# The entry of a hybrid encoder step: four chunks instead of three for the first three weight tiles, and the norm written out part by part

## The chip, the cores and the metric

The kernel runs on one NeuronCore of one Trainium2 chip, in a single launch. The metric is device time in microseconds (us): 1714.21 us, median of three runs (1712.94 to 1715.49). TensorE does matrix products, VectorE (DVE) and ScalarE (ACT) elementwise work, GpSimd (POOL) slower elementwise work, and SyncE (SP) issues most DMAs. Tiles with 128 partitions hold the data; TensorE writes to PSUM banks of 128x512 fp32.

## The reference, cut to what matters

One layer of a hybrid trunk on 1024 prompt tokens and 32 sample tokens, width 1024:

```python
h = rmsnorm(x, ln_mix_g)                 # per token: x * rsqrt(mean(x*x) + 1e-6) * g
z = h @ w_in + b_in                      # 1024 -> 2952 columns, split among head groups
x += w_out @ concat[mLSTM(z), stick_breaking_attention(z), S5(z) + GLU]
x += cross_attention(rmsnorm(x), memory K/V)
x += conv_ffn(rmsnorm(x))
y = rmsnorm(x, ln_f_g)
```

Everything is fp32. The kernel gets fp32 accuracy from the faster fp32r matmul by splitting each operand into a high part (rounded to fp32r) and a low part (the rest): a product is hi·hi + hi·lo + lo·hi, three matmuls.

## The kernel before, in words

The change lies in the entry, the first 64 us, in which the norm of x and the first three weight tiles of `w_in` are worked through.

**Token tiles.** x comes in nine token tiles (eight of 128 tokens, one of 32), `xts[0]` to `xts[8]`, loaded by `x_load` (L584) on SP's queue. `norm_T` (L555) takes one tile through: ACT squares it and sums over the row (L563); DVE computes mean + eps (L565); POOL raises that to the power -1/2 (L566); DVE multiplies x by this factor and by the weight row `gmix` in one instruction over 1024 columns (L568); TensorE turns the tile in two halves of four 128x128 transposes (L574); ACT copies each half from PSUM to `h_hi` as fp32r (L575), and DVE subtracts that from the PSUM half to give `h_lo` (L576). `gmix` is the weight row `ln_mix_g` repeated on all 128 partitions, loaded by one DMA of 512 KB (L593).

**Weight tiles.** `WStream` (L384) loads tiles of 1024 rows x 128 columns (512 KB, `w_raw`, two buffers). `split` (L406) makes `w_hi` on ACT (L417) and `w_lo` by a subtraction, on POOL for the first three tiles and on DVE afterwards (L418). The third tile holds the eight gate columns, and its two parts lie side by side in one operand, so that it takes two matmuls per row block instead of three.

**The product.** `dense_cmajor` (L464) runs the first three weight tiles (`u` 0, `u` 1, gate) chunk by chunk: the tokens are cut at `IN_AT` = 0, 384, 768, 1056 (L41), and each chunk needs its token tiles (`need_h`, L1684). `group` (L439) does one weight tile on one chunk: eight row blocks, 24 matmuls (16 for the gate). `ev_in` (L713) takes the result from PSUM to SBUF and DRAM. All other 21 weight tiles of `w_in` follow tile by tile (`dense`, L455).

**What sets the order.** The functions are generators. A planner written in the kernel keeps a modelled time for each engine (`place`, L72; `Timed`, L132): main work is written out in order, and after every second row block `advance` (L234) lets each side job (`Side`, `Window`, L189 to L227) write its next step if the modelled TensorE time has come to the step's due time. `x_tile` for the nine tiles runs in such a window of four at a time (L1680); the weight vectors that are needed later (`vec_late`, L638), the S5 part, stick-breaking attention, mLSTM and the memory norm are added as side jobs after eight steps of the main loop (L1710). The framework's scheduler (switched on in L2517) then sets the final order on each engine, so an instruction that is written later can be issued earlier if it is ready in the scheduler's model: three S5 loads on ACT's queue are issued at 0.73 to 1.66 us though S5 is written much later.

**Queues.** SP issues, in the order written (L592 to L618): x tile 0, `gmix`, x tiles 1 and 2, weight tile 0, x tile 3, weight tile 1, two bias rows, the gate bias, the gate weights, x tiles 4 to 8.

Of the kernel before, what the change touches and what calls it, by code (L numbers as in the profile page):

```python
# [39 lines left out]
IN_ORDER = "b0 b1 a0 a1 b2 a2".split()  # L40
IN_AT = [0, 3 * P, 6 * P, TA]  # L41


# [10 lines left out]
def tile_fn(tc, *args):  # L54
# [77 lines left out]
    class Timed:  # L132
# [23 lines left out]
        def __getattr__(self, name):  # L156
            f = getattr(self.eng, name)

            def timed(*args, **kw):
# [13 lines left out]
                return f(*args, **kw)  # L173
            return timed

    v = Timed(nc.vector, "dve")
# [5 lines left out]
    def asf(ap):  # L182
        return ap.bitcast(F32)
# [77 lines left out]
    with ExitStack() as top:  # L261
# [104 lines left out]
        def const(shape, dt=F32, name="c"):  # L366
            return cpool.tile(shape, dt, name=name)
# [16 lines left out]
        class WStream:  # L384
# [51 lines left out]

        W = WStream()

        def group(w, mov, c, n, kt):  # L439
# [147 lines left out]

        def x_tile(i):
            yield from norm_T(None, P if i < 8 else TS, gmix, h_hi, h_lo, i * P, xts[i])
            xn[0] = i + 1  # L590

        x_load(0, sy)  # L592
        sy.dma_start(gmix, a["ln_mix_g"][0].partition_broadcast(P))  # L593
        x_load(1, sy)
        x_load(2, sy)
        W.load()
        x_load(3, sy)
        W.load()


# [6 lines left out]
        def rows(tl, at, ap):  # L607
            n = ap.shape[0] // P
            sy.dma_start(tl[at:at + n, :], ap.rearrange("(r c) -> r c", c=P))
            return at + n  # L610

        rows(ra, rows(ra, 0, a["b_in"][0, 0:1536]), a["b_in"][0, 1544:2952])
        bgate = const([36, 1], name="bgate")
        sy.dma_start(bgate[0:4, :], a["b_in"][0, 1536:1540].unsqueeze(1))
# [23 lines left out]
        def vec_late():  # L638
# [74 lines left out]
        def ev_in(jj, c, ps):  # L713
            key, j = order[jj]
            sl = slice(IN_AT[c], IN_AT[c + 1])
            w = IN_AT[c + 1] - IN_AT[c]
            rs_ = slice(j * P, (j + 1) * P)
            pv = ps[:, :w]
            if key == "u":
                if c == 0:  # L720
                    full[jj] = xb.tile([P, 8, NB], "ur")
                n0, nn = IN_AT[c] // 8, w // 8
                s.activation(full[jj][:, :, n0:n0 + nn], pv.rearrange("p (n t) -> p t n", t=8), AF.Identity,
                             bias=vecA[:, bias_at[key, j]:bias_at[key, j] + 1])
                if c == NCH - 1:
                    sy.dma_start(d_u[rs_], full[jj])
                    avail.add((key, j))
                return
            clear(1)
            st = sp.tile([P, IN_W], "stg")[:, :w]  # L730
            if key == "gate":
# [7 lines left out]
                sy.dma_start(d_g[4:8, sl], st[32:36, :])  # L739
                if c == NCH - 1:  # L740
                    avail.add(key)
# [13 lines left out]
            if key in ("qa", "ka"):  # L755
                sy.dma_start((d_qa if key == "qa" else d_ka)[rs_, sl], st)
                if c == NCH - 1:
                    ready_a.append((key, j))
            if key in ("kb", "vb", "va", "oa"):
# [3 lines left out]
                def later():  # L763
                    ps2 = tp()
                    b0, nb = IN_AT[c] // P, w // P
                    for i in range((w + P - 1) // P):
# [3 lines left out]
                    v.tensor_copy(nat[:, b0:b0 + nb, :], ps2[:, 0:nb, :])  # L770
                    if c == NCH - 1:
                        v.tensor_copy(nat[:TS, 8, :], ps2[:TS, nb, :])
# [902 lines left out]

        hm = lambda k, c: (h_hi[:, k, IN_AT[c]:IN_AT[c + 1]], h_lo[:, k, IN_AT[c]:IN_AT[c + 1]])
        in_n = [IN_AT[c + 1] - IN_AT[c] for c in range(NCH)]
        chunks = list(range(NCH))
        h_free = []
        xw_ = add(Window((x_tile(i) for i in range(9)), 4))  # L1680
        until(lambda: xn[0] >= 1)
        W.prime(1)

        def need_h(c):  # L1684
            until(lambda: xn[0] * P >= min(IN_AT[c + 1], T) and (c < 2 or xn[0] == 9))

# [25 lines left out]
        drive(dense(len(order) - 3, hm, chunks, in_n, lambda j, c, ps: ev_in(j + 3, c, ps)))  # L1712
        clear(0)
# [807 lines left out]
```

## Time and profile before

| what | value |
|---|---|
| median of three runs | 1714.21 us |
| profiled execution, its own time | 1716.38 us |
| its span | 1714.6 us |
| granted TensorE clock, mean | 0.987 |
| PE busy | 1642.7 us, 96% of the span |
| DVE busy | 1137.3 us, 66% |
| ACT busy | 753.6 us, 44% |
| POOL busy | 463.2 us, 27% |

The profile is of one execution. Busy times of PE overlap from one matmul to the next, so the spacing of two starts tells a matmul's cost, not its duration. A row of the timeline gives the start and the length in us, the engine, the output and the inputs, the shape, how many instructions were merged, and in brackets how long the engine had been idle and what ended that. Tiles appear under the names of the memory zones in which they lie: `zb` holds `h_hi`, `za` holds `h_lo`, `zf` x tiles 0 to 3, `zy` x tiles 4 to 8, `zr` the gate weights' two parts.

### The profile page before, as it was taken

To read this page: it belongs to the slowest core of one execution; us is meant where nothing else is said; L and a number is where in the kernel's file an instruction comes from. 1 tells how busy PE (TensorE), PEld (TensorE's weight loads), DVE (VectorE), ACT (ScalarE), POOL (GpSimd) and SP (SyncE) were. 2 spreads that over 40 slices of the span, in tenths; PEclk is the share of its full clock that TensorE was granted. 3 is DMA by queue.
4 is the path that set the end of the run, shared out by engine and by line. 5 is a ranking of instruction groups with operands and counts; after the bars stand their busy time and mean duration, and the time that the engine had idled before them with its cause. 6 is when DMAs were issued, how large, how long until landed. Compare 5 with 4: busy or idle time off the path is not lost.

```text
span 1714.6 us, 30434 instructions
## 1 busy us (share of the span) xinstructions
PE 1642.7 (96%) x11616; PEld 1598.1 (93%) x11616; DVE 1137.3 (66%) x2209; ACT 753.6 (44%) x1480; POOL 463.2 (27%) x624
## 2 busy tenths in 40 slices
PE   5999999999999799999999989999999999999997
PEld 5989989999888799999999889999999999999997
DVE  6778878845796667766656698777777777333232
ACT  5434434534664555544444454444444445111143
POOL 4234335011214233200102546533333330000022
PEclk9999999999899999999999999999999999999999
DMA  7564544254479965455554555222222217332121
GB/s 216 146 161 115 138 109 105 78 158 133 124 232 257 253 200 162 125 170 178 171 167 124 159 158 169 94 76 89 86 75 75 76 63 240 127 100 75 43 69 65
DMA packets 328392, 229.91 MB, mean 134 GB/s; under 512 B 43564, under 2 KB 309707, under 8 KB 327991
## 3 DMA queue, kind: packets, MB, share of 16 engines
q1 hardware_dynamic: 309991, 214.57, 42.5%
q10 hardware_dynamic: 18256, 13.40, 2.6%
q8 instruction: 92, 1.51, 0.4%
q14 instruction: 53, 0.43, 0.1%
HBM read 170.95 MB, written 56.38 MB: 133 GB/s over the span
## 4 chain that ended last, share of the span: by engine, by line
PE 76%; DMA 9%; DVE 8%; issue 2%; ACT 2%; POOL 1%; SPq 1%; ACTq 0%; DVEq 0%; POOLq 0%
PE mm L173 47%; PE gp L173 19%; PE tp L173 10%; DVE zy L173 3%; DVE zf L173 2%; DVE zr L173 1%; DVE zx L173 1%; DMA d_mv<-zr 1%; DMA zf<-d_act 1%; SPq L173 1%; DVE w_lo L173 1%; DMA w_raw<-in_w_in_dram 1%; ACT zy L173 1%; DMA zy<-d_uu 1%; ACT zf L173 0%
## 5 line engine op out<-in xcount | busy, mean ns | idle before, releaser
L173 PE MATMUL mm<-zb,w_hi 128*128 128x352 f32 (+4 forms) x1234 | 366.5, 330 | 2.5 <-DVE zb L173 1.3
L173 PE MATMUL mm<-zr,w_hi 128*128 128x352 f32 (+2 forms) x1358 | 289.2, 312 | 8.4 <-ACT zf L173 4.1
L173 ACT ACTIVATE w_hi<-w_raw 128x1024 fp32r<-128x1024 f32 (+1 forms) x150 | 149.6, 997 | 284.5 <-PE mm L173 207.2
L173 PE MATMUL mm<-zb,w_lo 128*128 128x384 f32 (+2 forms) x826 | 273.6, 331 | 0.0
L173 POOL TENSOR_TENSOR zf<-zf 128x352 f32<-128x352 f32 (+5 forms) x98 | 118.5, 1210 | 566.5 <-ACT zf L173 484.8
L173 PE MATMUL mm<-zr,w_lo 128*128 128x264 f32 (+2 forms) x1058 | 235.9, 304 | 0.7 <-ACT zf L173 0.7
L173 PEld LDWEIGHTS mm<-zb,w_hi 128*128 128x128 f32 x1234 | 227.6, 190 | 4.3 <-DVE zb L173 1.6
L173 PEld LDWEIGHTS mm<-zr,w_hi 128*128 128x128 f32 x1358 | 216.2, 191 | 10.8 <-ACT zf L173 4.8
L173 DVE TENSOR_TENSOR w_lo<-w_raw,w_hi 128x1024 fp32r<-128x1024 f32 (+1 forms) x127 | 159.8, 1258 | 55.8 <-ACT w_hi L173 55.1
L173 PE MATMUL mm<-za,w_hi 128*128 128x384 f32 (+1 forms) x552 | 184.5, 334 | 0.0
L173 DVE TENSOR_TENSOR zx<-mm,zx 128x352 f32<-128x352 f32 (+3 forms) x120 | 62.7, 523 | 177.7 <-PE mm L173 177.3
L173 PEld LDWEIGHTS mm<-zr,w_lo 128*128 128x128 f32 x1058 | 164.6, 189 | 0.9 <-ACT zf L173 0.9
L173 PEld LDWEIGHTS mm<-zb,w_lo 128*128 128x128 f32 x826 | 157.8, 191 | 0.7
L173 PE MATMUL tp<-ident,zf 128*128 128x128 f32 (+3 forms) x530 | 89.1, 285 | 31.1 <-DVE zf L173 22.2
L173 PE MATMUL mm<-zy,w_hi 128*128 128x352 f32 x456 | 114.1, 326 | 1.6 <-DVE zx L173 1.6
L173 PE MATMUL gp<-zy 128*128 128x132 f32 (+13 forms) x722 | 109.7, 290 | 2.2 <-DVE zg L173 0.9
L173 DVE TENSOR_TENSOR zy<-zy 128x16 f32<-128x16 f32 (+9 forms) x371 | 97.5, 304 | 15.3 <-POOL zy L173 6.7
L173 ACT ACTIVATE zf<-gp 128x512 f32<-128x512 f32 (+6 forms) x180 | 75.6, 476 | 72.2 <-PE gp L173 59.6
L173 PEld LDWEIGHTS mm<-za,w_hi 128*128 128x128 f32 x552 | 106.4, 193 | 0.5
L173 PEld LDWEIGHTS tp<-ident,zf 128*128 128x128 f32 (+3 forms) x530 | 64.3, 146 | 41.7 <-DVE zf L173 20.8
L173 PEld LDWEIGHTS gp<-zy 128*128 128x128 f32 (+6 forms) x722 | 97.1, 186 | 4.9 <-DVE zg L173 1.3
L173 POOL TENSOR_TENSOR zy<-zy 128x16 f32<-128x16 f32 (+8 forms) x123 | 82.3, 680 | 67.7 <-DVE zy L173 56.9
(232 smaller groups left out, 3364.2 us busy)
## 6 DMA issues: line engine op xcount, KB each, us to landing
w_raw<-in_w_ffn_a_dram SPq DMA_DIRECT2D x27, 512.0 KB
w_raw<-in_w_out_dram SPq DMA_DIRECT2D x24, 512.0 KB
w_raw<-in_w_xq_dram SPq DMA_DIRECT2D x24, 512.0 KB
w_raw<-in_w_xo_dram SPq DMA_DIRECT2D x24, 512.0 KB
w_raw<-in_w_in_dram SPq DMA_DIRECT2D x23, 512.0 KB
d_act<-zx SPq DMA_DIRECT2D x22, 528.0 KB
zf<-d_act SPq DMA_DIRECT2D x22, 528.0 KB
w_raw<-in_w_ffn_down_dram SPq DMA_DIRECT2D x16, 512.0 KB
```

The source lines that it names most:

```text
L173: return f(*args, **kw)
```

## The change

- `IN_FIRST` = 0, 256, 512, 768, 1056: the first three weight tiles run over four chunks of two token tiles each (the last also has the 32 sample tokens). The other weight tiles keep `IN_AT`.
- The 512 KB load of `gmix` is gone. One row of 4 KB is loaded into a corner of `xts[7]`, TensorE multiplies a column of ones by it into two PSUM banks (`gps`), tiles 0 and 1 are scaled from PSUM, and ACT copies `gps` to `gmix` for the other tiles.
- SP's order is x 0, the weight row, x 1, the bias rows, weight tiles 0 and 1, x 2, x 3, then the rest as before.
- The norm is written out as parts (`squares`, `factor`, `scaled`, `turned`, `low`), for tiles 0 and 1 in a fixed interleaving, for the others in a generator that works on three tiles at a time. `keep` ties each of these instructions on ACT and DVE behind the one kept before on the same engine.
- `w_lo` of weight tile 0 is made on POOL in four quarters, of weight tile 1 on DVE in the kept order, of the gate tile on DVE.
- `vec_late` waits until 12 us of modelled TensorE time have gone by before it writes its two transposes, and these keep their place in the written order.

```diff
+IN_FIRST = [0, 2 * P, 4 * P, 6 * P, TA]
+    kept = {}
+    def keep(eng, name, *args, **kw):
+        if eng.key in kept:
+            with tc.issue_after(kept[eng.key]):
+                r = getattr(eng, name)(*args, **kw)
+        else:
+            r = getattr(eng, name)(*args, **kw)
+        kept[eng.key] = r.ins
...
-                s.activation(hi[:, :kt, :cols], raw[:, :kt, :cols], AF.Copy)
-                (v if self.at + len(self.ready) > 2 else g).tensor_tensor(
-                    out=lo[:, :kt, :cols], in0=raw[:, :kt, :cols], in1=asf(hi[:, :kt, :cols]), op=ALU.subtract)
+                if self.at + len(self.ready) < 2:
+                    keep(s, "activation", hi[:, :kt, :cols], raw[:, :kt, :cols], AF.Copy)
+                    if self.at + len(self.ready) == 0:
+                        for k in range(0, kt, 2):
+                            g.tensor_tensor(out=lo[:, k:k + 2], in0=raw[:, k:k + 2], in1=asf(hi[:, k:k + 2]),
+                                            op=ALU.subtract)
+                    else:
+                        keep(v, "tensor_tensor", out=lo[:, :kt, :cols], in0=raw[:, :kt, :cols],
+                             in1=asf(hi[:, :kt, :cols]), op=ALU.subtract)
+                else:
+                    s.activation(hi[:, :kt, :cols], raw[:, :kt, :cols], AF.Copy)
+                    v.tensor_tensor(out=lo[:, :kt, :cols], in0=raw[:, :kt, :cols], in1=asf(hi[:, :kt, :cols]),
+                                    op=ALU.subtract)
...
         x_load(0, sy)
-        sy.dma_start(gmix, a["ln_mix_g"][0].partition_broadcast(P))
+        grow = xts[7][0:1, :]
+        sy.dma_start(grow, a["ln_mix_g"][0].unsqueeze(0))
         x_load(1, sy)
-        x_load(2, sy)
-        W.load()
-        x_load(3, sy)
-        W.load()
         rows(ra, rows(ra, 0, a["b_in"][0, 0:1536]), a["b_in"][0, 1544:2952])
+        W.load()
+        W.load()
+        x_load(2, sy)
+        x_load(3, sy)
+        gps = [gp() for _ in range(2)]
+        for q in range(2):
+            pe.matmul(gps[q], ones4[0:1, :], grow[:, 512 * q:512 * q + 512], start=True, stop=True)
...
-            yield
+            t = clk["pe"]
+            while clk["pe"] < t + 12:
+                yield
             pa, pb = gp(), gp()
-            pe.transpose(pa[:, :34], ra[:34], ident[:34, :34])
-            pe.transpose(pb[:, :88], rb, ident[:88, :88])
+            tc.keep_in_program_order(pe.transpose(pa[:, :34], ra[:34], ident[:34, :34]))
+            tc.keep_in_program_order(pe.transpose(pb[:, :88], rb, ident[:88, :88]))
...
+        squares(0)
+        squares(1)
+        factor(0)
+        scaled(0, 0)
+        factor(1)
+        scaled(0, 1)
+        p00, p01 = turned(0, 0), turned(0, 1)
+        scaled(1, 0)
+        low(0, 0, p00)
         W.prime(1)
+        scaled(1, 1)
+        low(0, 1, p01)
+        p10, p11 = turned(1, 0), turned(1, 1)
+        low(1, 0, p10)
+        low(1, 1, p11)
+        xn[0] = 2
+        for q in range(2):
+            keep(s, "activation", gmix[:, HALF[q]], gps[q], AF.Copy)
+
+        def others():
+            for i in range(2, 11):
+                if i < 9:
+                    squares(i)
+                if 2 <= i - 1 < 9:
+                    scaled(i - 1)
+                if i < 9:
+                    factor(i)
+                yield
+                for q in range(2) if 2 <= i - 2 < 9 else ():
+                    low(i - 2, q, turned(i - 2, q))
+                    if q:
+                        xn[0] = i - 1
+                    yield
...
-        main = dense_cmajor(3, hm, chunks, in_n, ev_in, need_h)
+        main = dense_cmajor(3, hm(IN_FIRST), range(4), in_n(IN_FIRST), ev_in, need_h)
```

`squares`, `factor`, `scaled`, `turned` and `low` are L563, L565 with L566, L568, L574 with L575, and L576 of `norm_T`, with ACT's and DVE's instructions under `keep`; `scaled` of tiles 0 and 1 works on halves of 512 columns and reads `gps`, of the others on 1024 columns and reads `gmix`. `ev_in` takes its cuts from `IN_FIRST` for the first three weight tiles and asks for the last chunk by `last_c` instead of `NCH - 1`.

## Rows read from the trace of the kernel before

**Rows 1.** Stretches: length, busy us of each engine (instructions), granted clock, DMA share, GB/s.
```profile
0.00:22.40 22.40, 7.04 (x27) 5.27 (x28) 11.37 (x17) 12.61 (x20) 15.67 (x41) 1.00 0.86 267
22.40:63.67 41.27, 39.07 (x252) 36.88 (x251) 27.19 (x82) 24.22 (x47) 14.47 (x17) 1.00 0.46 124
63.67:640.00 576.33, 548.67 (x3865) 521.77 (x3863) 424.08 (x933) 285.24 (x646) 161.68 (x273) 0.97 0.58 160
```
**Rows 2.** Timeline of PE, first 26 us.
```profile
8.74 1.11 PE L173 MATMUL tp<-ident,zf 128*128 128x128 f32 x4 [8.74 <-DVE zf L173]
...
16.50 1.01 PE L173 MATMUL mm<-zb,w_hi 128*128 128x384 f32 x2 [1.17 <-ACT zb L173]
19.98 2.79 PE L173 MATMUL tp<-ident,zf 128*128 128x128 f32 x12 [2.47 <-DVE zf L173]
22.42 0.67 PE L173 MATMUL mm<-za,w_hi 128*128 128x384 f32 x1
...
24.46 0.33 PE L173 MATMUL mm<-za,w_hi 128*128 128x384 f32 x1
...
25.33 0.33 PE L173 MATMUL mm<-za,w_hi 128*128 128x384 f32 x1
```
**Rows 3.** Timeline of PE, 26 to 64 us.
```profile
26.02 0.60 PE L173 MATMUL tp<-ident,zf 128*128 128x128 f32 x4
...
30.63 0.45 PE L173 MATMUL gp<-ident,zy 34*128 34x34 f32 x2 [2.08 <-DMA zy<-in_ln_ffn_g_dram]
...
63.54 0.30 PE L173 MATMUL mm<-za,zr 128*128 128x288 f32 x1
```
**Rows 4.** Timeline of ACT, first 12 us.
```profile
4.54 1.06 ACT L173 ACTIVATE za<-zf 128x1024 fp32r<-128x1024 f32 x1 [1.86 <-DMA zf<-in_x_prompt_dram]
...
8.39 1.06 ACT L173 ACTIVATE za<-zf 128x1024 fp32r<-128x1024 f32 x1 [2.70 <-DMA zf<-in_x_prompt_dram]
...
10.81 0.58 ACT L173 ACTIVATE zb<-tp 128x512 fp32r<-128x512 f32 x1
11.51 1.06 ACT L173 ACTIVATE w_hi<-w_raw 128x1024 fp32r<-128x1024 f32 x1
```
**Rows 5.** Timeline of DVE, first 20 us.
```profile
5.72 0.15 DVE L173 TENSOR_SCALAR zf<-zf 128x1 f32<-128x1 f32 x1 [5.72 <-ACT za L173]
...
7.40 1.28 DVE L173 SCALAR_TENSOR_TENSOR zf<-zf 128x1024 f32<-128x1024 f32 x1
...
11.68 0.68 DVE L173 TENSOR_TENSOR za<-tp,zb 128x512 fp32r<-128x512 f32 x1
...
16.46 3.38 DVE L173 SCALAR_TENSOR_TENSOR zf<-zf 128x1024 f32<-128x1024 f32 x1 [0.51 <-POOL zf L173]
```
**Rows 6.** Timeline of POOL, first 20 us.
```profile
5.96 0.57 POOL L173 TENSOR_TENSOR zf<-zf,mhalf 128x1 f32<-128x1 f32 x1 [0.35 <-DVE zf L173]
...
16.40 2.35 POOL L173 TENSOR_TENSOR w_lo<-w_raw,w_hi 128x1024 fp32r<-128x1024 f32 x1
```
**Rows 7.** Timeline of PE: fp32 products of 264 columns, then fp32r products of 264 columns.
```profile
387.90 2.05 PE L173 MATMUL gp<-zy 128*128 128x264 f32 x8
389.59 0.49 PE L173 MATMUL mm<-zb,w_lo 128*128 128x288 f32 x1
...
971.75 3.07 PE L173 MATMUL mm<-zr,w_hi 128*128 128x264 f32 x24
974.66 1.61 PE L173 MATMUL mm<-zr,w_lo 128*128 128x264 f32 x12
```
**Rows 8.** SP's queue, then the chain of waits (start, us, what), first 16 us.
```profile
4.70 0.34 SPq L173 DMA_DIRECT2D zf<-in_x_prompt_dram  x1
...
5.08 9.80 DMA w_raw<-in_w_in_dram
```
**Rows 9.** The stretch 550 to 600 us, then one step of the chain in it.
```profile
550.00:600.00 50.00, 37.50 (x293) 35.14 (x293) 29.83 (x62) 25.07 (x76) 14.36 (x15) 0.93 0.94 251
...
583.57 8.53 DMA d_mv<-zr
```

More of the change, by code (lines that the diff above doesn't have):

```diff
@@ L437, in tile_fn @@
         W = WStream()
+        HALF = [slice(0, 512), slice(512, D)]
         def group(w, mov, c, n, kt):
@@ L586, in x_load @@
             eng.dma_start(xts[i][:n], a["x_prompt"][0, i * P:i * P + n, :] if i < 8 else a["x_sample"][0])
[L588 to L592, printed above, removed]
-        sy.dma_start(gmix, a["ln_mix_g"][0].partition_broadcast(P))
-        x_load(1, sy)
-        x_load(2, sy)
-        W.load()
-        x_load(3, sy)
-        W.load()
         VA = {}
@@ L714, in ev_in @@
             key, j = order[jj]
-            sl = slice(IN_AT[c], IN_AT[c + 1])
-            w = IN_AT[c + 1] - IN_AT[c]
+            at = IN_FIRST if jj < 3 else IN_AT
+            sl = slice(at[c], at[c + 1])
+            w = at[c + 1] - at[c]
+            last_c = c == len(at) - 2
             rs_ = slice(j * P, (j + 1) * P)
@@ L1673, in glu, with hm, in_n @@
             yield
-        hm = lambda k, c: (h_hi[:, k, IN_AT[c]:IN_AT[c + 1]], h_lo[:, k, IN_AT[c]:IN_AT[c + 1]])
-        in_n = [IN_AT[c + 1] - IN_AT[c] for c in range(NCH)]
+        def hm(at):
+            return lambda k, c: (h_hi[:, k, at[c]:at[c + 1]], h_lo[:, k, at[c]:at[c + 1]])
+        def in_n(at):
+            return [at[c + 1] - at[c] for c in range(len(at) - 1)]
         chunks = list(range(NCH))
         h_free = []
-        xw_ = add(Window((x_tile(i) for i in range(9)), 4))
@@ L1681, in tile_fn, with width_of, squares, factor @@
-        until(lambda: xn[0] >= 1)
-        W.prime(1)
+        sss = {}
+        def width_of(i):
+            return P if i < 8 else TS
+        def squares(i):
+            n = width_of(i)
+            xt = xts[i][:n]
+            ss = sss[i] = sp.tile([P, 3], "ss")
+            sq = h_lo[:, :, i * P:(i + 1) * P] if n == P else xb.tile([P, KD, P], "mhl", F32R)
+            keep(s, "activation", sq[:n], xt.rearrange("p (k c) -> p k c", k=KD), AF.Square, accum_out=ss[:n, 0:1])
+        def factor(i):
+            n = width_of(i)
+            ss = sss[i][:n]
+            keep(v, "tensor_scalar", ss[:, 1:2], ss[:, 0:1], 1.0 / D, EPS, op0=ALU.mult, op1=ALU.add)
+            g.tensor_tensor(out=ss[:, 2:3], in0=ss[:, 1:2], in1=mhalf[:n], op=ALU.pow)
@@ new lines, in scaled, with turned @@
+        def scaled(i, q=None):
+            n = width_of(i)
+            sl = slice(0, D) if q is None else HALF[q]
+            x = xts[i][:n, sl]
+            keep(v, "scalar_tensor_tensor", x, x, sss[i][:n, 2:3], gps[q] if i < 2 else gmix[:n, sl], op0=ALU.mult,
+                 op1=ALU.mult)
+        def turned(i, q):
+            n = width_of(i)
+            ps = tp()
+            for j in range(4):
+                k = 4 * q + j
+                pe.transpose(ps[:, j, :n], xts[i][:n, k * P:(k + 1) * P], ident[:n, :n])
+            keep(s, "activation", h_hi[:, 4 * q:4 * q + 4, i * P:i * P + n], ps[:, :, :n], AF.Copy)
+            return ps
@@ new lines, in low @@
+        def low(i, q, ps):
+            n = width_of(i)
+            sl = (slice(None), slice(4 * q, 4 * q + 4), slice(i * P, i * P + n))
+            keep(v, "tensor_tensor", out=h_lo[sl], in0=ps[:, :, :n], in1=asf(h_hi[sl]), op=ALU.subtract)
+        squares(0)
[7 more added lines that the diff above has]
+        low(0, 0, p00)
+        W.prime(1)
+        scaled(1, 1)
@@ L1684, in need_h @@
+        add(others())
         def need_h(c):
-            until(lambda: xn[0] * P >= min(IN_AT[c + 1], T) and (c < 2 or xn[0] == 9))
+            until(lambda: xn[0] * P >= min(IN_FIRST[c + 1], T) and (c < 3 or xn[0] == 9))
         def lend():
@@ L1711, in tile_fn @@
                 later_sides()
-        drive(dense(len(order) - 3, hm, chunks, in_n, lambda j, c, ps: ev_in(j + 3, c, ps)))
+        drive(dense(len(order) - 3, hm(IN_AT), chunks, in_n(IN_AT), lambda j, c, ps: ev_in(j + 3, c, ps)))
         clear(0)
```

14 lines of the change are left out of this document (8 added, 6 removed).

## The prediction

> **What bounds the kernel now.** I read the stretches first: how busy TensorE (PE) is before and after the entry. Up to 22.40 us PE is busy for 7.04 us, so 15.36 are lost; from there to 63.67 us, where the first three weight tiles end (their last matmul starts at 63.54), 2.20 are lost; from 63.67 to 640 us 27.66 of 576.33 [rows 1, 3]. PE is the bound nearly everywhere, so what the entry wastes is paid in full, unless a later wait takes it back. Next PE's timeline, for what the loss in the entry consists of: the first transposes wait until 8.74 us, two product matmuls run at 16.50, then twelve transposes at 19.98 come first, and the product flows only from 22.42 [rows 2]. Later there is one hole, 2.08 us, where the vector transposes wait for a small DMA [rows 3]. Last come the timelines of ACT, DVE, POOL and SP, to see who is late. The second x tile has landed at 8.39, nearly 4 us after the first at 4.54, with the 512 KB weight row between them in the queue [rows 4]. The scaling of the fourth tile takes 3.38 us where another takes 1.28, while POOL's 2.35 us subtraction runs from 16.40 [rows 5, 6].
>
> **The change part by part.** I follow the new order until the product flows.
>
> *Norm row.* A 512 KB load goes, a 4 KB one comes. Tile 0 stays at 4.54; tile 1 lands when its own 512 KB have followed. The nearest rows bound this: not before tile 0, and not later than 8.39. At 267 GB/s, the mean of the stretch, 512 KB take 2.0 us; nothing else large is in the queue then, so I take 5.9. New on PE are two fp32 products of 512 columns. Four products of 264 columns in fp32 (two records each) take 389.59 - 387.90 = 1.69 us, 0.42 each, or 0.82 for 512 columns [rows 7]. PE is slow there: the first four transposes take 1.11 us against 0.60 later, at a granted clock listed as 1.00 (the 2.4 GHz level) in both stretches [rows 1 to 3]. So I take 1.65 each: the row lands with tile 0 at about 4.5, the halves are ready at 6.15 and 7.8. If they ran at the later speed they would be done at 6.15, which is the other end.
>
> *Tiles 0 and 1.* Factor 0 is ready at 5.96 + 0.57 = 6.53 [rows 6]; half 0 of tile 0 is scaled by 7.3 (0.68, as a 128x512 DVE instruction that reads PSUM [rows 5]); half 1 waits for the second bank, 7.9 to 8.55. PE, in order behind its two products, turns the halves 7.8 to 8.9 and 8.9 to 10.0. ACT copies them 9.0 to 9.6 and 10.1 to 10.7 (0.58 [rows 4]), then in the kept order makes `w_hi` of weight tile 0, 10.7 to 11.75 (1.06), and only then copies tile 1, 11.75 to 12.35 and 12.35 to 12.95. DVE alternates scaling and low parts at 0.68 each; the first low part of tile 1 is done at 13.1. POOL's quarters of `w_lo` (2.35/4, about 0.6 each) run 11.8 to 14.2, each ahead of its matmuls. So the product flows from about 13.1 instead of 22.42: 9.3 earlier. By 22.42 the old kernel had turned a third tile and done two matmuls, 2 x 0.36 + 2 x 0.174 = 1.07 us of PE work still to do: 8.2 left.
>
> *Chunks.* A matmul of 384 columns takes (25.33 - 24.46)/5 = 0.174 us once PE is fast, five starts lying between; one of 264 takes (974.66 - 971.75)/24 = 0.121 [rows 2, 7]. That is 0.45 ns per column and next to nothing fixed: 0.118 for 256, 0.132 for 288. Each chunk has 24 + 24 + 16 = 64 matmuls: before 64 x (2 x 0.174 + 0.132) = 30.7 us, after 64 x (3 x 0.118 + 0.132) = 31.1. I charge 0.5: 7.7 left; the bounds are 0 and 1.
> The Trainium skill speaks against narrow chunks: "TensorE: Matmul & The Clock Gate", section "Back-to-back issue gap", gives a sustained 81 ns per matmul at 128 columns and 131 ns at 512, a cost that is mostly fixed. An estimate on a straight line between them is 98 ns at 256 columns, 102 at 288 and 114 at 384, which makes the four chunks 25.3 us against 21.1, 4.2 dearer, so a time of some 1711.7. The rows do not agree (0.174 at 384, not 0.114), and I follow the rows.
>
> *A new hole.* Chunk 0 holds only two tiles. With weight tile 0 from 13.1 to about 16.7 (its first matmuls slow, some 0.7 more than warm), weight tile 1 (24 x 0.118 = 2.8) and the gate (1.9), PE is through at 21.4. Weight tile 1's `w_hi` follows two 0.58 copies of the norm row on ACT, 14.1 to 15.2; its `w_lo` on DVE, priced as the 1.28 row, ends at 16.5, in time. Only then does DVE's kept order come to tiles 2 and 3: gate low part to 17.1, factor and power 17.9, scaling 19.25, then tile 3's power and scaling 21.4, the two low parts of tile 2 22.95, scaling of tile 4 24.25, first low part of tile 3 25.1. Chunk 1 thus starts at 25.1; the four turns of tiles 2 and 3 (1.44) fill part of the 3.7, and 2.3 is lost. This and the slow first matmuls: 7.7 - 2.3 - 0.7 = 4.7 left. Bounds of the hole: 0, if the scheduler lets TensorE go on by halves, and 5, if ACT's squares of tile 4, kept ahead of tile 2's copies, wait for the tile's DMA. In steady state a tile costs DVE 0.15 + 1.28 + 2 x 0.68 = 2.8 us and a chunk of two PE 7.5, so chunks 2 and 3 do not wait.
>
> *Weight tile 1 and gate on DVE.* POOL no longer holds a long subtraction while DVE scales, which is where 3.38 instead of 1.28 came from [rows 5, 6]; that delay lay ahead of 22.42 and is in the sum already.
>
> *Vector transposes.* Written 12 us later and held in order, they find their rows landed: the hole of 2.08 goes, 6.8 left. At worst it stays as it was.
>
> Sum: 9.3 - 1.1 - 0.5 - 2.3 - 0.7 + 2.1 = 6.8 at the end of the third weight tile. All side jobs hang on what these tiles deliver, so I let the rest move up with PE, and take off 0.6 for waits that fall differently: 6.2. On the profiled execution (1716.38, span 1714.6) that gives 1710.2; it stands 2.17 above the median 1714.21, and against the median I forecast 1708.0. With the bounds above (hole 0 or 5, chunks 0 or 1, the old hole kept) the gain runs from 3 to 9.5: 1704.7 to 1711.2.
>
> **The rivals.**
> *Late weights.* The change would then not do what it says. SP's ninth DMA (tile 3) was issued only at 4.70, when an early load had landed; weight tile 1 behind it took 9.80 us from issue to landing [rows 8]. In the new order the ninth is weight tile 0, and ACT's kept order puts its `w_hi` before tile 1's copies. If it lands as late as that, at 14.5 instead of before 10.7, all that follows slips by 3.8, less the hole (the tiles behind it come closer): gain 3, 1711.2. Against it: only 1 MB of x goes ahead of it, where 3 MB went ahead of weight tile 1.
> *Taken back.* From 550 to 600 us PE loses 12.50 us while the DMA engines are 0.94 busy, with legs as long as 8.53 us in the chain [rows 9]. If transfers there cannot move up, PE waits that much longer: 1714.2. Against it: the stretch from 63.67 has a mean DMA share of 0.58, so there is room ahead.
> *Slower.* Side jobs are placed by the modelled PE clock, and four chunks and the 12 us shift that clock against every job's due time. In the same stretch, 550 to 600, a store and reload of the memory values (8.53) may come behind instead of beside PE's work: one more leg in series costs 8.5 and makes 1716.5, which still counts as taken back; two cost 17 and make 1725. It decides from the point where the 27.66 us that PE loses between 63.67 and 640 grow by more than 9.6, a third.
> *Narrow matmuls dearer*, as the quoted rule has it: in rows, 64 matmuls in each of four chunks at 16 ns more each than I charge, 4.1 us, so 1712; the rows of 264 columns leave it little.
>
> **How the numbers follow.** Chances: forecast 0.54 (its own range 1704.7 to 1711.2), late weights 0.12, taken back 0.17, slower 0.15, narrow matmuls 0.02. A change of 0.2%, 3.4 us, is about what a measurement of this kernel can tell. Faster by more than that (below 1710.8): 0.95 of the forecast and half of the late weights, 0.57. Slower by more (above 1717.6): the case of two legs, 0.15. Within 0.2%: 0.28. The range for 8 in 10 leaves out the two-leg end and a little below: 1704 to 1718.
>
> **What would show it.** In the changed profile: the first product matmul near 12.5 us, a steady flow from 13; tile 1's square near 6, not 8.4; a PE wait of 2 to 3 us near 22 to 25 on a DVE or ACT part of tile 2 or 3; no 2 us wait on the `ln_ffn_g` load; 256-column starts 0.118 apart; the last gate matmul near 57 instead of 63.5. I am wrong if that matmul is not at least 3.4 us earlier, if ACT waits for weight tile 0's load, or if PE's loss between there and `w_out` grows by more than a few us.

## The result: 47 us slower, not 6 us faster

The changed kernel takes 1761.31 us (median of four runs, 1757.19 to 1764.28), the kernel before on the same chip 1713.79 us (four runs, 1712.94 to 1715.49). The ratio is 1.0274, with a 95% interval of 1.0252 to 1.0297. I had forecast 1708.0 us and a range of 1704 to 1718.

The profiled execution of the changed kernel took 1764.28 us, with a span of 1762.2, 47.6 more than the span before. PE's matmuls are busy for 1664.9 us, 22.2 more than before, and PE is idle for 97.3 us instead of 71.9, 25.4 more. Of the 22.2, the norm row's products are 3.75; for the rest the products are over the same columns (in 64 more matmuls), and the mean granted clock is 0.972 instead of 0.987, which over such a span would be some 26 us (an estimate: 1762 x 0.015). So the loss is a good half waiting, and most of the rest is matmuls at a lower granted clock (its two levels are 1.2 and 2.4 GHz) in stretches in which PE has stood still.

The stretches of the changed kernel, against [rows 1] (length, busy us of each engine, granted clock, DMA share, GB/s):

```profile
0.00:22.40 22.40, 16.17 (x93) 12.65 (x93) 12.32 (x24) 15.42 (x28) 11.27 (x42) 1.00 0.79 246
22.40:63.67 41.27, 32.55 (x233) 31.43 (x234) 21.16 (x52) 18.88 (x39) 10.01 (x9) 0.88 0.34 89
63.67:640.00 576.33, 525.26 (x3620) 496.04 (x3619) 399.52 (x923) 273.98 (x611) 143.78 (x272) 0.95 0.55 150
```

PE now loses 6.23 us up to 22.40 (before 15.36), 9.13 less; 3.75 of these hold the norm row's own products, and the early start came. From 22.40 to 63.67 it loses 8.72 (before 2.20), and from there to 640 us 51.07 (before 27.66): 6.52 and 23.41 given away. The two losses have different causes.

**The entry.** PE's timeline of the changed kernel answers to [rows 2, 3]:

```profile
5.17 3.75 PE L174 MATMUL gp<-zy,ones 1*128 1x512 f32 x4 [5.17 <-DMA zy<-in_ln_mix_g_dram]
...
13.71 0.39 PE L174 MATMUL mm<-za,w_hi 128*128 128x256 f32 x1 [0.34 <-DVE za L174]
13.94 0.28 PE L174 MATMUL mm<-zb,w_lo 128*128 128x256 f32 x1
...
19.25 0.28 PE L174 MATMUL mm<-zb,w_lo 128*128 128x256 f32 x1
...
23.29 0.22 PE L174 MATMUL gp<-ident,zy 34*128 34x34 f32 x1 [0.97 <-DMA zy<-in_ln_ffn_g_dram]
...
29.98 0.38 PE L174 MATMUL gp<-ident,zy 88*128 88x88 f32 x1 [5.02 <-DMA zy<-in_ffn_conv_b_dram]
...
65.03 0.30 PE L174 MATMUL mm<-za,zr 128*128 128x288 f32 x1
```

The product flows from 13.71. But the vector transposes, which I had expected to wait no more, wait 0.97 + 5.02 = 6.0 us for their small DMAs instead of 2.08: PE comes to them some 9 us earlier, while SP issued the last of their rows at 24.61 instead of 26.57, only 2 earlier. Another 1.59 + 0.65 us are waits for ACT's and VectorE's parts of the last x tiles, ahead of the last chunk. After the long hole the clock goes down as well (windows of the changed kernel, same columns as above):

```profile
20.00:30.00 10.00, 4.01 (x34) 3.59 (x33) 4.45 (x9) 6.52 (x14) 1.45 (x3) 0.94 0.61 136
30.00:40.00 10.00, 9.43 (x60) 9.14 (x61) 5.53 (x10) 2.53 (x6) 1.10 (x2) 0.72 0.51 145
```

PE is busy for 4.01 of 10 us, and in the next 10 us the granted clock is 0.72, a mean between its two levels. The last matmul of the third weight tile starts at 65.03, later than before (63.54). Nothing of the early start is left at the end of the entry, and that is still not the 47.

**What comes late behind it.** In the timeline of VectorE of the changed kernel, the scaling of the last x tile (32 tokens), then the scaling of the first memory tile:

```profile
47.26 1.26 DVE L174 SCALAR_TENSOR_TENSOR zy<-zy,zf 32x1024 f32<-32x1024 f32 x1
...
52.09 1.28 DVE L174 SCALAR_TENSOR_TENSOR zf<-zf 128x1024 f32<-128x1024 f32 x1 [2.96 <-issue]
```

Before, these stood at 31.28 and 38.63. Both are some 13 to 16 us late. `mem_norm`, the norm of the 256 memory rows, is a side job that is written only when all nine x tiles are done and weight tile `u` 1 is through its last chunk. It stores its result in `d_mT`, and its buffers have to come back (`lend`) before the stick-breaking attention may start. The rows that follow are the last low parts (`h_lo`) of the x tiles on VectorE and the first transposes of the first memory tile on PE, in the kernel before:

```profile
48.19 0.29 DVE L173 TENSOR_TENSOR za<-tp,zb 128x128 fp32r<-128x128 f32 x1 [0.80 <-ACT zb L173]
50.76 1.09 PE L173 MATMUL tp<-ident,zf 128*128 128x128 f32 x8
```

and in the changed kernel:

```profile
54.17 1.09 DVE L174 TENSOR_TENSOR za<-tp,zb 128x512 fp32r<-128x512 f32 x3
86.94 0.60 PE L174 MATMUL tp<-ident,zf 128*128 128x128 f32 x4
```

The x tiles are finished 7 us later (55.3 instead of 48.5), the memory tile is turned 36 us later, though it is scaled by 53.4. So most of its delay arises behind the x tiles: before, its transposes stand right behind those of the last x tile; now they come only with the next transposes on PE. (In neither kernel does PE turn any tile for some 30 us behind that place: none starts between 51.8 and 83.5 before, and none between 54.9 and 84.9 now.) What makes them miss the earlier place no run shows.

SP's queue of the kernel before:

```profile
101.66 4.18 SPq L173 DMA_DIRECT2D d_mT<-zr  x2
105.88 1.88 SPq L173 DMA_DIRECT2D zr<-d_q  x2
```

and of the changed kernel:

```profile
97.09 1.06 SPq L174 DMA_DIRECT2D d_mT<-zr  x1
...
119.67 1.45 SPq L174 DMA_DIRECT2D d_mT<-zr  x2
...
123.92 1.32 SPq L174 DMA_DIRECT2D zr<-d_q  x2
```

The first memory tile is stored at 97.09 (before 53.2), the second at 119.67 (101.66), and the stick-breaking's second load of q stands right behind that, 18 us later than before. VectorE, which works off the side jobs, is busy for 69.25 us between 50 and 150 us instead of 80.29. S5's first result is stored at 181.5 instead of 156.2, the mLSTM's gates (`d_uu`) at 460.1 instead of 426.9.

**Where PE pays.** From 430 to 520 us PE has the last weight tiles of `w_in` (the last matmul starts at 479.12 instead of 467.57), side jobs, and then the first products of the memory's keys and values (`mm<-zm`). There, in the kernel before:

```profile
430.00:460.00 30.00, 28.86 (x194) 26.05 (x194) 19.35 (x34) 18.74 (x41) 7.50 (x8) 0.84 0.41 106
460.00:490.00 30.00, 26.95 (x188) 23.78 (x187) 26.49 (x35) 18.65 (x42) 7.36 (x19) 0.94 0.73 220
490.00:520.00 30.00, 29.86 (x262) 29.15 (x262) 27.77 (x49) 20.19 (x51) 3.51 (x5) 1.00 0.78 231
```

and in the changed kernel:

```profile
430.00:460.00 30.00, 25.53 (x154) 22.65 (x153) 16.48 (x21) 15.66 (x28) 2.11 (x3) 1.00 0.28 91
460.00:490.00 30.00, 21.39 (x110) 17.83 (x111) 24.45 (x37) 14.66 (x30) 6.10 (x9) 0.71 0.54 164
490.00:520.00 30.00, 26.25 (x187) 24.15 (x187) 14.83 (x30) 23.52 (x48) 5.92 (x14) 0.78 0.57 147
```

PE does some 450 matmuls there instead of 640, at a clock of 0.71 and 0.78 in the last two thirds, and loses 16.8 of 90 us instead of 4.3. That is 12.5 of the 23.4 us; 6.2 more are lost from 520 to 640 us, 3.1 from 100 to 150. Its waits from 425 to 520 us are 16.8 us in all, before 5.7. Most are those of side jobs that stand in its queue; the second line is the products of the memory's keys and values, which wait for `d_mT` to be loaded again (engine, tile written, what it waited for: us, times, longest):

```profile
PE tp L174 <- POOL zf L174: 4.5, 1, 4.5
PE mm L174 <- DMA zm<-d_mT: 3.4, 2, 2.6
PE gp L174 <- ACT zf L174: 2.7, 2, 1.6
PE tp L174 <- DVE zr L174: 2.7, 1, 2.7
PE tp L174 <- DVE zy L174: 2.0, 1, 2.0
```

The longest of these waits shows how a late side job holds up products:

```profile
464.00 1.12 PE L174 MATMUL tp<-ident,zf 128*128 128x128 f32 x4 [4.52 <-POOL zf L174]
...
473.86 0.59 PE L174 MATMUL mm<-zb,w_hi 128*128 128x288 f32 x1
```

The matmul at 473.86 begins the last chunk of the last weight tile of `w_in`. PE had used the same weights for the chunk before from 452.52 on, and yet this chunk comes only behind the transposes, for which PE stood idle 4.52 us. The in-projection's last store, `d_oa`, which the mLSTM reads, is issued at 518.6 instead of 482.7, the mLSTM's last store at 663.0 instead of 623.8, 39 later.

### The profile page after: what moved, and what is told of

Same layout as the page of the kernel before. It is cut to its first block, busy times and chain, and to the rows that moved or that the text cites. A ratio compares the mean times of both kernels' runs of the same rounds, so it can differ in the third digit from the quotient of the medians.

```text
span 1762.2 us, 30621 instructions
## 1 busy us (share of the span) xinstructions
PE 1664.9 (94%) x11684; PEld 1615.9 (92%) x11684; DVE 1131.6 (64%) x2215; ACT 759.4 (43%) x1492; POOL 445.5 (25%) x625
## 4 chain that ended last, share of the span: by engine, by line
PE 53%; DVE 5%; DMA 5%; ACT 1%; issue 1%; POOL 0%; SPq 0%; DVEq 0%; POOLq 0%; ACTq 0%
PE mm L174 33%; PE gp L174 13%; PE tp L174 7%; DVE zx L174 2%; DMA zf<-d_act 1%; DVE zr L174 1%; DMA zy<-d_uu 1%; DVE zy L174 1%; DVE w_lo L174 1%; DVE zb L174 1%; DMA w_raw<-in_w_ffn_down_dram 0%; DVE zf L174 0%; ACT zr L174 0%; DVE w_hi L174 0%; DMA zf<-d_e 0%
## 5 line engine op out<-in xcount | busy, mean ns | idle before, releaser
L174 PE MATMUL mm<-zb,w_hi 128*128 128x352 f32 (+4 forms) x1250 | 372.2, 331 | 2.9 <-ACT zb L174 1.8
L174 PE MATMUL mm<-zb,w_lo 128*128 128x384 f32 (+4 forms) x842 | 276.8, 329 | 0.0
L174 POOL TENSOR_TENSOR zf<-zf 128x352 f32<-128x352 f32 (+5 forms) x98 | 114.7, 1172 | 588.3 <-ACT zf L174 497.6
L174 PEld LDWEIGHTS mm<-zb,w_hi 128*128 128x128 f32 x1250 | 233.0, 192 | 5.1 <-ACT zb L174 2.1
L174 PE MATMUL mm<-za,w_hi 128*128 128x384 f32 (+2 forms) x568 | 186.8, 329 | 0.9 <-DVE za L174 0.9
L174 PEld LDWEIGHTS mm<-zb,w_lo 128*128 128x128 f32 x842 | 162.6, 193 | 0.6
L174 PEld LDWEIGHTS mm<-za,w_hi 128*128 128x128 f32 x568 | 110.6, 195 | 2.0 <-DVE za L174 1.4
L174 DVE TENSOR_TENSOR zy<-zy 128x16 f32<-128x16 f32 (+10 forms) x371 | 96.2, 300 | 17.7 <-POOL zy L174 9.1
L174 PE MATMUL tp<-ident,zf 128*128 128x128 f32 (+1 forms) x530 | 88.1, 284 | 16.2 <-POOL zf L174 4.5
L174 PE MATMUL gp<-zr 128*128 128x256 f32 (+3 forms) x384 | 81.3, 338 | 13.8 <-DMA zr<-d_q 5.6
```

## The experiments

Theory A: the vector transposes, written later and held in their place, and the hole that they make in the entry are to blame. Theory B: the side jobs are planned otherwise. After the first four runs B was split. M: the memory norm comes late, because the x tiles ahead of it do, and holds up what waits for its buffers. K: the pinned order of `keep` does it. P: a shifted plan does it, whatever the memory norm does. All runs below were single, each beside a run of the kernel before on the same chip (1713.55, 1714.79, 1715.80, 1713.73 and 1714.46 us for the five groups). In the table the third weight tile ends where its last matmul starts, the other columns are the starts of stores, in us; in brackets stands the copy that takes the place of the memory norm.

| kernel | 3rd weight tile ends | `d_mT` first, last | `d_oa` last | mLSTM's last store | time |
|---|---|---|---|---|---|
| before | 63.5 | 53.2, 105.3 | 482.7 | 623.8 | 1713.79 |
| after | 65.0 | 97.1, 120.3 | 518.6 | 663.0 | 1761.31 |
| after, `vec_late` as before | 65.6 | 98.1, 120.8 | 518.6 | 660.2 | 1764.3 |
| before, `vec_late` as after | 63.6 | 52.8, 104.6 | 486.0 | 627.5 | 1716.04 |
| after, three chunks | 64.0 | 96.0, 120.7 | 508.7 | 652.0 | 1753.38 |
| before, side jobs after 12 steps | 64.2 | 53.8, 104.2 | 482.2 | 623.4 | 1714.14 |
| after, no kept order | 66.3 | 100.0, 123.7 | 520.7 | 662.1 | 1761.59 |
| after, old window | 64.0 | 54.2, 116.4 | 499.2 | 661.5 | 1743.22 |
| before, memory norm late | 62.8 | 101.6, 126.0 | 492.7 | 657.0 | 1746.93 |
| after, memory store on ACT | 63.2 | 93.3, 117.4 | 514.3 | 656.1 | 1759.61 |
| after, no memory norm | 63.8 | (30) | 506.7 | 647.2 | 1733.38 |
| before, no memory norm | 61.9 | (32) | 475.4 | 622.4 | 1719.33 |
| after, three chunks, old window | 75.7 | 57.4, 113.5 | 510.0 | 649.8 | 1742.63 |
| before, four chunks | 68.2 | 52.6, 111.2 | 499.7 | 639.5 | 1739.37 |
| after, three chunks, no memory norm | 63.5 | (27) | 506.6 | 650.7 | 1739.31 |
| before, norm row and loads of after | 63.8 | 53.4, 104.6 | 484.1 | 625.8 | 1715.85 |
| before, S5 late | 62.2 | 55.9, 97.7 | 493.1 | 639.9 | 1728.07 |
| before, short mLSTM | 64.1 | 53.7, 105.3 | 483.1 | 610.8 | 1719.17 |
| after, three chunks, a tile per turn | 59.0 | 56.3, 96.5 | 507.9 | 650.8 | 1746.57 |
| after, a tile per turn | 61.6 | 52.5, 98.2 | 485.6 | 623.5 | 1721.27 |

The column of the third weight tile says little about the last one. The column of `d_oa` goes with it, and tells where a loss has arisen, not why: the seven kernels in which it stands at 486.0 or earlier (the one before among them) take 1713.8 to 1721.3 us, all those at 492.7 or later 1728.1 to 1764.3.

**1. The late vector transposes, undone in after and done alone in before.**

```diff
-            t = clk["pe"]
-            while clk["pe"] < t + 12:
-                yield
+            yield
```

> The changed kernel with the vector transposes written as before (no wait of 12 us of modelled time, no fixed place in the written order); all else as changed. Theory A, pinned transposes: the 6.0 us that PE stands still at 23 to 30 us (0.97 and 5.02), the slow matmuls after them and the late ScalarE and S5 work that follows are the cause; then the third weight tile ends near 57 to 59 us instead of 65, and the total is 1708 to 1718. Theory B, replanned side jobs: the entry gets 5 to 8 us better, but S5, memory norm and mLSTM stay in the changed order, PE still starves between 440 and 650 us, and the total stays above 1740.

> The kernel before with only the vector transposes changed (12 us of modelled time later, in their written place). Theory A: PE's wait there grows from 2.1 to 5 us or more, work behind it is late, and the total rises by 10 to 45 us, to 1725 to 1760. Theory B: the place of two transposes alone hardly moves the side jobs; PE loses or gains at most 3 us and the total is 1708 to 1720.

Measured 1764.3 and 1716.04. Writing the transposes later neither costs nor gains; the hole in the entry stays when they are written as before (4.02 + 0.83 us), since the rows themselves are late for a PE that starts 9 us earlier. Theory A falls.

**2. Three chunks in after; side jobs added later in before.**

```diff
-IN_FIRST = [0, 2 * P, 4 * P, 6 * P, TA]
+IN_FIRST = IN_AT
```

```diff
-            if n_main == 8:
+            if n_main == 12:
```

> The changed kernel with the first three weight tiles over the old three chunks (384, 384, 288 columns); all else as changed. Theory A: the pinned transposes still stop PE for several us, total 1750 to 1770. Theory B, with the four chunks as what shifts the plan: the side jobs come back to about their old places, total 1710 to 1730.

> The kernel before with one number changed: the side jobs (late vectors, S5, memory norm, attention, mLSTM) join after 12 steps of the main loop instead of 8, some 4 us of PE time later. Nothing else is touched. Theory A: no long stop of PE arises, total within 5 us of 1713.8. Theory B: the order of the side jobs alone is worth tens of us, and the total moves by 8 us or more, up or down.

Measured 1753.38 and 1714.14. Without the four chunks 40 us of the loss remain, and the plan before bears a later start of all side jobs at no cost. So the plan is not upset by just any shift.

**3. No kept order.** `keep` only calls the instruction, without `issue_after`.

> The changed kernel without the kept order: the entry is written as in the change, but nothing pins ScalarE's and VectorE's instructions to the order in which they are written. Theory K (the pinned order of the two engines is what holds the tiles 2 to 8 and all behind them back): the loss goes, 1705 to 1720 us, the last token tile is scaled near 31 us as before. Theory M (the tiles 2 to 8 are written one after the other, in steps of which one is issued per turn, so the memory norm behind them starts late, and everything that waits for its memory with it): still 1750 to 1765 us, the first store to d_mT near 97 us.

Measured 1761.59: no change. The rows that tell most are VectorE's scaling of the last x tile in this kernel and its last low parts of the x tiles, and beside them the stores of the memory norm:

```profile
32.50 1.27 DVE L174 SCALAR_TENSOR_TENSOR zy<-zy,zf 32x1024 f32<-32x1024 f32 x1
...
54.22 1.09 DVE L174 TENSOR_TENSOR za<-tp,zb 128x512 fp32r<-128x512 f32 x3 [0.21 <-ACT zb L174]
```

```profile
L174 SPq DMA_DIRECT2D d_mT<-zr x4: 570/712/1020, 100.0 to 123.7; - x4
```

The last tile is scaled as early as before (31.28), but its transposes and low parts come as late as in the changed kernel (54.17), and the memory norm is as late too. So it is neither the pinned order nor the scaling that holds the x tiles and the memory norm back. Theory K falls, and M stands, as its expectation had it (1750 to 1765 us, first store near 97): what is left is that tiles and norm are written late, in the plan (tested in 9).

**4. Tiles 2 to 8 by the old generator; the memory norm held back in before.**

```diff
-        add(others())
+        add(Window((x_tile(i) for i in range(2, 9)), 4))
```

```diff
+            t = clk["pe"]
+            while clk["pe"] < t + 20:
+                yield
             yield from mem_norm()
```

> The changed kernel with tiles 0 and 1 as in the change, but tiles 2 to 8 by the old generator, four tiles open at a time. Theory M: the last token tile is scaled near 31 us again, the first store to d_mT comes near 53 us, S5's first result before 160 us, and the time falls to 1703 to 1718 us. Theory P (four chunks and a shifted plan misplace the side jobs, whatever the tiles do): stays above 1740 us with d_ys near 180 us.

> The kernel before with one thing alone added: the memory norm is held back by 20 us of the plan's clock before it starts; token tiles and everything else as before. Theory M: the first store to d_mT moves from 53 to beyond 75 us, the stick-breaking's second q load behind 115 us, d_ys behind 170 us, and the time rises to 1735 to 1765 us. Theory S (S5's own memory, which holds the token tiles 4 to 8, or the plan as a whole is the cause): the time stays within 1709 to 1722 us.

Measured 1743.22 and 1746.93. The late memory norm alone makes the kernel before slower by 32 us, as theory M has it, though S5's first result did not come later there (148.6 against 156.2): of the path that I had written down, the step over S5 was wrong, and the one over the stick-breaking's loads right (130.4 us). The old window brought the first memory tile back to 54.2, but not the second, and only 18 of the 47 us. So an early first memory tile is not enough.

**5. The memory norm's stores on ScalarE's queue.**

```diff
-                sy.dma_start(asf(d_mT[0][:, :, i * P:(i + 1) * P]), asf(mh))
+                s.dma_start(asf(d_mT[0][:, :, i * P:(i + 1) * P]), asf(mh))
```

> The changed kernel with the four stores of the memory norm (d_mT) issued by ScalarE's queue instead of SP's. If the in-order SP queue behind those stores is the link by which the late memory norm delays the stick-breaking's q load (123.9 us against 105.9 us before): that load falls below 112 us and the time to 1715 to 1740 us. If the link is the memory that the norm gives back late, or the plan: the load stays beyond 118 us, the time at 1750 to 1770 us.

Measured 1759.61, with the second q load at 120.4. SP's order is not the link.

**6. No memory norm, in after, in before and with three chunks.**

```diff
-            yield from mem_norm()
+            for i in range(2):
+                sy.dma_start(asf(d_mT[i][:]), asf((h_hi, h_lo)[i][:, :, 0:NMEM]))
+            yield
```

> The changed kernel without the norm of the 256 memory rows: what is stored in d_mT is a copy of the first 256 normed tokens instead, so the cross attention's keys and values are of other data; everything else is computed. Theory M (the memory norm's second tile, stored at 119.7 us in the changed kernel and at 101.7 in the one before, holds the stick-breaking's second q load, and with it S5, the stick-breaking and the mLSTM): the second q load falls below 106 us, the mLSTM's last store from 663 to below 635 us and the time to 1700 to 1725 us. Rival P (four chunks and a shifted plan misplace the side jobs whatever the memory norm does): d_ys stays beyond 170 us, the time above 1740 us.

> The kernel before without the norm of the memory rows, in the same way. Theory M: if the second q load hangs on the memory norm there too (105.9 us, right behind the norm's store at 105.3), it moves forward by 5 to 15 us and the time falls to 1695 to 1712 us. Rival P: 1711 to 1717 us; the work removed is some 16 transposes and a few us of ScalarE and VectorE beside PE.

> The changed kernel with three chunks and without the norm of the memory rows (d_mT holds a copy of the first 256 normed tokens). If the late memory norm and the four chunks are the whole loss, the time comes back to that of the kernel before without the norm: 1712 to 1724 us, the last mLSTM store at 618 to 632 us. If the written-out tiles 2 to 8 cost something of their own: 1727 us and more.

Measured 1733.38, 1719.33 and 1739.31. In the changed kernel 28 us come back; in the kernel before nothing is gained, though the second load of q there moved from 105.9 to 83.1 us, so that load being earlier is not worth anything by itself. So the late memory norm is a large part of the loss, and not all of it. With three chunks the rest is larger, not smaller, against what I expected: late memory norm and four chunks do not add up to the loss.

**7. The other parts alone.** The chunks alone in before; of after, three chunks with the old generator; and the norm row and the DMA order alone in before.

```diff
+IN_FIRST = [0, 2 * P, 4 * P, 6 * P, TA]
-        main = dense_cmajor(3, hm, chunks, in_n, ev_in, need_h)
+        main = dense_cmajor(3, hm(IN_FIRST), range(4), in_n(IN_FIRST), ev_in, need_h)
```

```diff
+        for q in range(2):
+            pq = gp()
+            pe.matmul(pq, ones4[0:1, :], grow[:, 512 * q:512 * q + 512], start=True, stop=True)
+            s.activation(gmix[:, 512 * q:512 * q + 512], pq, AF.Copy)
```

> The kernel before with the four chunks for the first three weight tiles and nothing else of the change. If the four chunks shift the plan by themselves: second memory tile stored beyond 110 us, d_ys beyond 168 us, the time 1730 to 1750 us. If they are harmless without the rest: 1708 to 1720 us.

> The changed kernel with three chunks and with tiles 2 to 8 by the old generator: of the change the DMA order, the norm row by TensorE, the two written-out tiles and the late vector transposes stay. Theory M with the chunks as the second cause of what the old window alone left (1743.2 us): first d_mT near 53 us, second q load at 104 to 110 us, d_ys at 152 to 160 us, the time 1705 to 1718 us. Rival (the DMA order or the written-out tiles themselves disturb the plan): stays at 1730 to 1750 us.

> The kernel before with the entry part of the change alone: its DMA order (two weight tiles ahead of the third token tile) and the norm row spread by TensorE and copied by ScalarE; tiles by the old generator, three chunks. The product flow starts earlier than 22.4 us (my estimate 16 to 19) and the third weight tile ends at 58 to 62 us instead of 63.5. If an earlier entry is worth its time: 1707 to 1712 us. If the side chain ends when it did, because it does not hang on the first products: 1712 to 1717 us. If the new order moves the memory norm or the side jobs: above 1725 us.

Measured 1739.37, 1742.63 and 1715.85. Four chunks alone cost 24 us, though 14 products of the first chunk run earlier (from 15.37; the flow still starts at 22.40) and the memory norm's first store is not late (52.6). The norm row and the new order of loads alone do not bring the flow forward (two matmuls at 22.95, the flow from 24.44) and leave the time as it was.

**8. S5 held back; a shorter mLSTM.** Both in before: a wait of 25 us as in 4, ahead of S5's first step; and without the norm over the heads at the end of each mLSTM chunk.

> The kernel before with S5 alone held back by 25 us of the plan's clock; tiles, memory norm, chunks as before. If the side chain S5, GLU, mLSTM has no slack: the last mLSTM store goes from 624 to beyond 640 us and the time to 1730 to 1750 us. Rival (S5 has slack, and only the stick-breaking, which waits for the memory norm's buffers, decides): 1710 to 1720 us.

> The kernel before without the norm over each head at the end of every mLSTM chunk: four squares on ScalarE, one power on GpSimd and two small VectorE instructions less per chunk, nothing less on PE. If the side chain that ends with the mLSTM's last store sets the time: that store comes at 598 to 618 us instead of 624 and the time falls to 1690 to 1709 us. Rival (PE's own stream sets the time up to 640 us, the chain follows it): 1711 to 1716 us.

Measured 1728.07 and 1719.17. With S5's first result 44 us later the time is 14 us longer, less than expected: that path has slack. And a chain that ends 13 us earlier (610.8) makes nothing faster. My reading that the end of the mLSTM sets the time falls: it is late where the time is long, but its own length is not the bound.

**9. Tiles 2 to 8 a whole tile per turn**, with three chunks and with four.

```diff
                 if i < 9:
                     factor(i)
-                yield
                 for q in range(2) if 2 <= i - 2 < 9 else ():
                     low(i - 2, q, turned(i - 2, q))
                     if q:
                         xn[0] = i - 1
-                    yield
+                yield
```

> The changed kernel with three chunks and with the tiles 2 to 8 issued a whole tile per turn instead of a third of one. If the pace of these turns is what holds the tiles back: the last tile is scaled before 40 us (48.1 with three steps per tile), the first store to d_mT comes before 75 us (96 us), and the time falls from 1753 to 1712 to 1735 us. Rival (the order in which they are written, not the pace, holds them: each tile's VectorE and ScalarE steps stand between PE's products): the last tile still beyond 44 us, the time at 1740 to 1760 us.

> The changed kernel as it is, with four chunks, and with the tiles 2 to 8 issued a whole tile per turn. If the pace is the cause: 1720 to 1745 us, with the four chunks' own cost left (24 us when they stand alone). Rival (order, not pace): 1750 to 1765 us.

Measured 1746.57 and 1721.27. With everything else of the change in place, this gives back 40 of the 47 us. The stretches of this kernel (four chunks):

```profile
0.00:22.40 22.40, 16.59 (x94) 13.14 (x95) 12.36 (x24) 15.49 (x27) 11.23 (x42) 1.00 0.81 247
22.40:63.67 41.27, 35.44 (x264) 33.67 (x263) 28.10 (x86) 23.60 (x47) 12.68 (x17) 0.96 0.50 136
63.67:640.00 576.33, 545.77 (x3853) 519.48 (x3852) 416.48 (x928) 287.40 (x647) 159.97 (x273) 0.97 0.58 159
```

The last stretch is nearly as before: 30.56 us lost, not 51.07. The stores of the memory norm:

```profile
L174 SPq DMA_DIRECT2D d_mT<-zr x4: 547/593/708, 52.5 to 98.2; - x4
```

The first memory tile is turned at 47.43 again, right behind the last x tile:

```profile
47.43 1.09 PE L174 MATMUL tp<-ident,zf 128*128 128x128 f32 x8
```

For the change as it stands this names the cause of most of the loss: the number of turns that tiles 2 to 8 take in the plan. In the change the generator `others` yields 23 times, one step per turn, here 9 times, where the old window took a step of up to four tiles in each turn; all jobs that ask for nine finished tiles are written behind that.

With three chunks the same edit gives back only 7 us, though the entry there ends at 59.03 and the memory norm's last store (96.5 us) and the second q load (99 us) are earlier than before. PE then loses 46.2 us from 63.67 to 640, 18.6 more than before, and 16.4 of these from 460 to 520 us, just behind the last product of `w_in` (458.55):

```profile
460.00:490.00 30.00, 18.18 (x118) 16.32 (x118) 15.98 (x21) 18.89 (x35) 3.85 (x12) 0.77 0.58 175
490.00:520.00 30.00, 22.27 (x157) 20.03 (x155) 23.46 (x33) 16.18 (x39) 2.64 (x7) 0.89 0.51 145
```

with 13.7 us of waits of transposes on VectorE between 425 and 520 us. That is about the place at which the changed kernel pays too. So a late memory norm alone is enough to cost some 30 us (4, in the kernel before), but an early one does not save a plan that is changed elsewhere.

**What stays open.** Which side job's step comes to stand ahead of the last products, and why, when only the chunks change (24 us) or with three chunks and quick tiles (32 us). The effects of the parts do not add: the old window (4), with an early first memory tile too, gives back 18 us and not 40, so how much of the 40 lies in the turns alone and how much in a plan that happens to fit is not shown. No version beat the kernel before.

## Why the prediction was wrong

- *Start of the flow.* Forecast 13.1, measured 13.71; tile 1 squared at 6.43 (forecast 5.9); the two norm-row products 3.75 us (forecast 2 x 1.65); at 22.40 PE is ahead by 64 products of 256 columns less the two of 384, 64 x 0.118 - 2 x 0.174 = 7.2 us of work (forecast 8.2, or 7.5 with its slow first matmuls). This part was right, and "late weights" did not happen: `w_hi` of weight tile 0 began at 11.40. (The "ninth DMA" of that rival is SP's sixth; it is the ninth with the three on ACT's queue.)
- *Narrow matmuls.* Starts 0.118 apart at 256 columns (13.94 to 19.25, 45 spacings), as read from [rows 2, 7]. The rule of the Trainium skill quoted there ("TensorE: Matmul & The Clock Gate", section "Back-to-back issue gap"), by which the spacing would be an estimated 98 ns, does not hold for these matmuls.
- *Vector transposes.* "They find their rows landed: the hole of 2.08 goes." It grew to 6.0. The transposes are written 12 us of the plan's clock later, but PE is 9 us earlier, and I had not followed the rows themselves: SP issued those of `ffn_conv_w` at 22.6 to 24.0 us, and those of `ffn_conv_b` at 24.61. I had also priced a hole as idle time alone, not the granted clock of 0.72 behind it. With the new hole of 2.3 that I had expected in its place, the entry should have ended near 57 and ended at 65.03.
- *The step that failed*: "All side jobs hang on what these tiles deliver, so I let the rest move up with PE." They hang on turns of the plan, and I had not counted these: 23 in the new generator. Tiles 0 and 1 came earlier, the last tile was scaled 16 us and finished 7 us later, and the memory norm's first store came 44 us later. Of the 47 us, 40 come back when the number of turns alone is changed (1721.27).
- *The rival "slower".* Its kind was right (side jobs placed by a shifted plan) and so was its deciding point: PE's loss from 63.67 to 640 grew by 23.4, more than 9.6. Its place and price were wrong. I had looked at 550 to 600 us, two more legs, 17 us. 12.5 of the 23.4 us fall between 430 and 520 us, and the price was nearly three times as high. One reason is the clock: of the 47.6 us, 22.2 are more busy time of PE, 3.75 of them the norm row's products and most of the rest matmuls at a lower granted clock.
- *The range.* The bounds named do not give 3 to 9.5: all adverse ones together (hole 5, chunks 1, the old hole kept) make 6.2 - 2.7 - 0.5 - 2.1 = 0.9, all good ones 9.0. The miss lies far outside either.
- *What a good entry would be worth* stays open. In the kernel with a tile per turn PE loses 11.6 us up to 63.67 instead of 17.6, but 3.75 of these 5.9 are the norm row's own products, and the third weight tile ends only 1.9 us earlier (61.63). The whole is no faster (1721.27 against 1714.46): 2.9 are lost again before 640, and its PE is busy for 4.9 us longer. No run has both an entry that ends near 57 and the old plan behind it, so the rival "taken back" is neither shown nor refuted.

## What to carry to other kernels

Where main work and side jobs are interleaved by a plan, count the turns that a rewritten step takes, and look up every job that waits for its last part; a step that begins earlier but ends later delays them all, and here 7 us later became 36 for the job behind it. A queue that is worked off as written turns a late side job into idle time of the engine that was to be kept busy, far from the place of the change, and a lower clock behind it adds to the price (here some 18 us to 25). A tuned interleaving has no sum of parts: measure a part both alone in the old kernel and undone in the new one before a cause is named.

## What the runs showed of the hardware that I had not expected

A product with one row and 512 fp32 columns takes 3.75/2 = 1.87 us on PE at the start of the kernel, though only one of the 128 rows of the operand holds data. PE is slow there for other work too, while the profile lists a granted clock of 1.00: in the kernel before with four chunks, products of 256 columns start 0.213 us apart from 16.31 to 18.44, against 0.118 later. And waits cost more than their own length: over the whole execution, 25.4 us more of idle PE came with 22.2 us more of busy PE, of which only 3.75 are products that were not there before.
